# State space mixer in fp32: masks added in the exponent, the two directions' decays summed, states multiplied with C itself

## The chip, the cores and the metric

The kernel runs on 1 core of one Trainium2 chip. The metric is the device time of one execution in microseconds (us); "before" is the median of 3 runs. The engines are TensorE (PE; its weight loads are PEld), VectorE (DVE), ScalarE (ACT), GpSimd (POOL) and SyncE (SP, which issues most DMAs).

## The reference, cut to what matters

The model has two layers; the change lies in the second layer's mixer, a bidirectional state space mixer (Mamba-2 form) over 512 latent tokens that start from a state built by 256 context tokens. There are 8 groups of 4 heads; a head has 64 channels and a group one B and one C of 128 state rows per token. Per direction and chunk:

```python
acum = jnp.cumsum(dtc * a, axis=2)
seg = acum[:, :, :, None] - acum[:, :, None, :]
decay = jnp.exp(jnp.where(causal, seg, -jnp.inf))
cb = jnp.einsum('nblgk,nbsgk->nblsg', cc, bc)
y_diag = jnp.einsum('nblsgh,nbsghp->nblghp', cb[..., None] * decay * dtc[:, :, None], xc)
...
y = y_d + jnp.einsum('blgk,bghpk->blghp', c_i, hs) * jnp.exp(a_i)[..., None]
...
y = (yf + yb + dsk * xs).reshape(bsz, t, SSD_INNER) * jax.nn.silu(z.astype(F32))
yg = yg * lax.rsqrt(jnp.mean(yg * yg, axis=-1, keepdims=True) + RMS_EPS)
```

`yf` and `yb` are the two directions; the norm runs over the 256 channels of a group. An output projection, a residual and an expert layer with 16 experts follow.

## The kernel before, in words

One program in the Tile framework; the framework places each engine's instructions in an order of its own from the program's order and a simulated timeline, and each engine then works through its queue in that order. Tiles come from pools with a fixed number of buffers; an instruction or load that needs a buffer waits until its last reader is done. PSUM has 8 banks: tags "mm" (3), "tp" (2), "at" (2) and "o" (1).

The mixer (L1389 to L1655) works on chunks of 128 tokens: 4 latent chunks and 2 of context. **Setup** (L1414 to L1476): the step sizes dt of 64 head-directions, their cumulated decays `ac` (64 x 768), written to DRAM as `acd` (L1468); `ad` = ac - ln dt; both transposed to `acT` and `adT` (tokens on partitions); the chunk ends go to DRAM and come back broadcast as `eb` (L1469), whose exponential ScalarE takes (L1471).

**Per group** (loop at L1517): the input projection on TensorE for x, B, C and later z, each product in three passes of split fp32r (the weights are split by ScalarE and VectorE, L721 and L722); the 5-tap convolution, four taps of it on VectorE (L1492); transposes; `cb`, the product of B and C of a chunk, with each direction's triangle multiplied in by VectorE (L1563); `xw`, x times its weight, on GpSimd (L1572); the chunk states `st` in a chain of three steps over TensorE, GpSimd (L1585) and VectorE (L1589, L1597).

**Per block** m of two heads (128 channels; 2 blocks a group) and direction d, L1613 to L1642: `R` is a load of two heads' cumulated decays, broadcast to all partitions (L1621, issued by ScalarE's queue; 2 buffers). Eight VectorE instructions of 128x128 make the exponent `mt` = min(R, acT) - adT (L1627), ScalarE takes the exponential (L1629), VectorE multiplies with `cb` (L1630), and 8 matmuls with 64 columns of weights each add x·mt to `py`. ScalarE also takes exp(R) (L1631), GpSimd multiplies it with C (L1632), and 8 matmuls of the same shape add st·R to `py`. Every fp32 matmul shows as two records in the trace.

After both directions VectorE reads `py` (L1646), multiplies with the gate (L1648), and ScalarE squares (L1649). A group's norm (`norm_group`, L1499) runs in the middle of the next group's projection: 8 matmuls with a column of ones sum the squares, then a power on GpSimd, transposes, and the scaled y goes to DRAM `yd`, from which the output projection (`project`, L1673) reads it back. All of the helper `mm`'s matmuls have line L77.

## Time and profile before

| | us |
|---|---|
| median of 3 runs | 2380.43 |
| lowest and highest | 2377.44 and 2381.2 |
| profiled execution, its own time | 2382.69 |
| span of the profiled execution | 2381.0 |
| its mean granted TensorE clock | 0.979 of full speed |

The rows below come from the profiled execution, so a sum over them stands against its own time. Busy time says how long an engine worked in a stretch; the chain of waits says which work the end waited for; "idle before" beside a group of instructions says how long its engine stood still before them and which instruction ended that.

### The profile page before, as it was taken

The page shows a single profiled execution, that of the slowest core. Times are in us where ns is not written, and L with a number is a line of the kernel's source. Part 1 is how long each engine was busy: PE and PEld are TensorE (multiplying, and loading weights), DVE is VectorE, ACT ScalarE, POOL GpSimd, SP SyncE. Part 2 cuts the span into 40 slices and gives each one's busy share as a digit, 9 for nine tenths or more (in the row PEclk, how much of TensorE's full clock was granted, in tenths as well). Part 3 has the DMA queues.
Part 4 walks back from the last instruction along what each step waited for, and adds up shares of the span by engine and source line. Part 5 has one row for each costly group of instructions (what it writes and reads, how often), then busy time and mean ns, then how long its engine had stood idle before and what let it go on. Part 6 is the DMA issues. An engine that isn't in the chain of part 4 may idle for free. (4 is left out here: it accounts for less than half of the span.)

```text
span 2381.0 us, 37608 instructions
## 1 busy us (share of the span) xinstructions
PE 2228.0 (94%) x15522; PEld 1392.7 (58%) x15522; DVE 1273.3 (53%) x2231; ACT 847.0 (36%) x1408; POOL 513.9 (22%) x383
## 2 busy tenths in 40 slices
PE   7999999989999999999988999999989999988886
PEld 6888887877344444444476787777768633322222
DVE  5566476635243443343577888888885512222224
ACT  4446455522242343343463444434443211111111
POOL 1000044421121222221222434334442000000001
PEclk9999999999899999999998999999999899999999
DMA  8554311249999999999733232322256999999996
GB/s 270 162 163 150 103 37 55 71 137 338 352 368 366 370 379 387 368 383 356 271 101 108 91 124 92 94 84 89 89 178 243 358 366 418 419 419 418 419 418 264
DMA packets 253707, 587.94 MB, mean 247 GB/s; under 512 B 14240, under 2 KB 129056, under 8 KB 253536
## 3 DMA queue, kind: packets, MB, share of 16 engines
q1 hardware_dynamic: 240960, 548.44, 61.2%
q0 software_dynamic: 5280, 18.88, 3.1%
q10 hardware_dynamic: 7296, 18.22, 2.3%
q8 instruction: 122, 2.00, 0.3%
q14 instruction: 49, 0.40, 0.1%
HBM read 560.99 MB, written 24.51 MB: 246 GB/s over the span
## 5 line engine op out<-in xcount | busy, mean ns | idle before, releaser
L77 PE MATMUL mm<-w_moe,xs 128*32 128x512 f32 (+1 forms) x4080 | 596.3, 597 | 20.7 <-DMA w_moe<-in_w_dram 20.7
L77 PE MATMUL mm<-xh,w_s 128*128 128x512 f32 (+2 forms) x1824 | 479.1, 357 | 4.4 <-ACT z L1087 3.7
L77 PEld LDWEIGHTS mm<-w_moe,xs 128*32 128x32 f32 (+1 forms) x4080 | 171.1, 116 | 397.9 <-issue 336.4
L77 PEld LDWEIGHTS mm<-xh,w_s 128*128 128x128 f32 (+1 forms) x1824 | 307.3, 189 | 55.9 <-issue 8.2
L77 PE MATMUL mm<-xl,w_s 128*128 128x512 f32 (+1 forms) x912 | 296.4, 357 | 0.0
L77 PEld LDWEIGHTS mm<-xl,w_s 128*128 128x128 f32 x912 | 160.0, 189 | 24.7 <-issue 4.2
L77 PE MATMUL at<-w_s,hT_h 128*96 128x512 f32 x480 | 162.8, 405 | 1.6 <-POOL w_s L514 1.1
L514 DVE TENSOR_TENSOR w_s<-w_moe,w_s 128x1024 fp32r<-128x1024 f32 x90 | 126.9, 1432 | 62.9 <-ACT w_s L513 62.6
L1492 DVE SCALAR_TENSOR_TENSOR acc<-u,cwh,acc 128x770 f32<-128x770 f32 (+1 forms) x128 | 149.2, 1173 | 15.2 <-ACT acc L1489 13.9
L514 POOL TENSOR_TENSOR w_s<-w_moe,w_s 128x1024 fp32r<-128x1024 f32 x30 | 75.0, 2499 | 334.1 <-ACT w_s L513 257.7
L513 ACT CAST w_s<-w_moe 128x1024 fp32r<-128x1024 f32 x120 | 124.4, 1049 | 46.7 <-PE at L77 22.1
L1632 POOL TENSOR_TENSOR R<-R,cT 128x1024 f32<-128x1024 f32 x32 | 101.3, 3179 | 132.2 <-ACT R L1631 109.6
L77 PE MATMUL at<-w_moe,o 128*64 128x512 f32 x512 | 119.9, 599 | 8.9 <-DMA w_moe<-in_w_dram 7.3
L479 DVE TENSOR_TENSOR ha<-mm,ha 128x512 f32<-128x512 f32 x16 | 11.1, 691 | 217.6 <-PE mm L77 216.9
L77 PEld LDWEIGHTS at<-w_s,hT_h 128*96 128x96 f32 x480 | 75.1, 161 | 59.3 <-issue 22.6
L478 ACT ACTIVATE ha<-mm 128x512 f32<-128x512 f32 x16 | 9.6, 597 | 260.1 <-PE mm L77 260.1
L772 DVE TENSOR_TENSOR w_s<-w_raw,w_s 128x1024 fp32r<-128x1024 f32 x56 | 75.7, 1357 | 46.3 <-ACT w_s L771 46.1
L77 PE MATMUL at<-w_s,hT_l 128*96 128x512 f32 x240 | 94.2, 392 | 0.0
L1572 POOL TENSOR_TENSOR xw<-xk,weT 128x256 f32<-128x256 f32 x80 | 72.3, 935 | 98.5 <-ACT xk L1550 98.5
L647 DVE TENSOR_TENSOR ha<-mm,ha 128x512 f32<-128x512 f32 x16 | 11.1, 691 | 147.7 <-PE mm L77 147.7
L77 PE MATMUL mm<-w_s,xh 128*128 128x256 f32 x480 | 89.2, 290 | 0.2
L646 ACT ACTIVATE ha<-mm 128x512 f32<-128x512 f32 x16 | 9.6, 597 | 223.6 <-PE mm L77 223.6
(463 smaller groups left out, 3680.1 us busy)
## 6 DMA issues: line engine op xcount, KB each, us to landing
w_moe<-in_w_dram SPq DMA_DIRECT2D x380, 1024.0 KB
w_ada<-in_ada_w_dram SPq DMA_DIRECT2D x34, 1024.0 KB
w_raw<-in_ssd_w_in_dram SPq DMA_DIRECT2D x16, 1024.0 KB
R<-acd ACTq DMA_DIRECT2D x32, 512.0 KB
spare<-in_ada_w_dram SPq DMA_DIRECT2D x14, 1024.0 KB
w_raw<-in_ab_w_in_dram SPq DMA_DIRECT2D x12, 1024.0 KB
w_raw<-in_ssd_w_in_dram SPq DMA_DIRECT2D x16, 512.0 KB
w_raw<-in_ssd_w_out_dram SPq DMA_DIRECT2D x8, 1024.0 KB
```

The lines of the kernel that those rows point to most:

```text
L77: return T.matmul(o, l, r, start=start, stop=stop, skip_group_check=True, **k)
L478: S.activation(ha, B[0], AF.Silu)
L479: V.tensor_tensor(ha, B[1], ha, ALU.mult)
L513: S.copy(wh, w2[:, kk, :])
L514: (G if k % 4 == 3 else V).tensor_tensor(wl, w2[:, kk, :], wh.bitcast(F32), ALU.subtract)
L646: S.activation(ha, B[0], AF.Silu)
L647: V.tensor_tensor(ha, B[1], ha, ALU.mult)
L772: V.tensor_tensor(wl, r, wh.bitcast(F32), ALU.subtract)
L1492: V.scalar_tensor_tensor(acc[:, :n], u[:, i:i + n], cwh[:, i * 32 + cblk:i * 32 + cblk + 1], acc[:, :n], op0=ALU.mult, op1=ALU.add)
L1572: G.tensor_tensor(xw[:, i, d, :].rearrange("p (h c) -> p h c", h=4), xk[:, i, :].rearrange("p (h c) -> p h c", h=4), we[:, i, d, :].unsque ...
L1632: G.tensor_tensor(R, R, cT.rearrange("p (a b) -> p a b", a=4).unsqueeze(1).to_broadcast([128, 2, 4, 128]), ALU.mult)
```

## The change

The triangle is no longer multiplied into `cb` but added to the exponent: `tri` holds 0 and -1e30. VectorE adds it to a whole `R` tile of 128x1024 at once, and ScalarE takes eight exponentials of 128x128 with `adN` = ln dt - ac as the bias. The two directions' decays are summed by VectorE before one product with the unmasked `cb` (copied from PSUM by ScalarE) and one set of 8 matmuls. The states are multiplied with C itself (4 matmuls with 128 columns of weights per direction, into an "at" or a "tp" bank), and VectorE scales that product by `E` = exp(ac), which the setup computes once, stores as `ead`, and each block loads broadcast to 64 partitions per head. GpSimd sums the two directions' E, adds the sum to y between VectorE's two instructions, and sums the squares of a group's two blocks, so that 4 matmuls do in place of 8. `R` has 3 buffers and is also the place of `mt`; `E` has 3.

```diff
--- before.py
+++ after.py
@@ -1389,14 +1389,15 @@
         w_in = A["ssd_w_in"]
         yd = dram.tile([16, 128, LAT], F32, name="yd")
         acd = dram.tile([64, LAT], F32, name="acd")
+        ead = dram.tile([64, LAT], F32, name="ead")
         lad = dram.tile([64, 4], F32, name="lad")
         with ExitStack() as sx:
             sp = sx.enter_context(tc.tile_pool(name="ssc", bufs=1, side="right"))
             tri = [sp.tile([128, 128], F32, name=f"stri{d}") for d in range(2)]
             for d in range(2):
                 sgn = 1 - 2 * d
-                G.memset(tri[d], 1.0)
-                G.affine_select(out=tri[d], in_=tri[d], pattern=[[sgn, 128]], compare_op=ALU.is_ge, fill=0.0,
+                G.memset(tri[d], 0.0)
+                G.affine_select(out=tri[d], in_=tri[d], pattern=[[sgn, 128]], compare_op=ALU.is_ge, fill=-1e30,
                                 base=0, channel_multiplier=-sgn)
             ones = sp.tile([128, 1], F32, name="ones")
             G.memset(ones, 1.0)
@@ -1405,8 +1406,7 @@
             V.tensor_scalar(cwh, vec("cw"), 0.5, None, op0=ALU.mult)
             V.tensor_scalar(cbh, vec("cb"), 0.5, None, op0=ALU.mult)
 
-            acT = sp.tile([128, NTL, 64], F32, name="acT")
-            adT = sp.tile([128, NTL, 64], F32, name="adT")
+            adN = sp.tile([128, NTL, 64], F32, name="adN")
             weT = sp.tile([128, NT, 64], F32, name="weT")
             eb = sp.tile([128, 64, 4], F32, name="eb")
             sp = sx.enter_context(tc.tile_pool(name="ssd", bufs=1, side="right"))
@@ -1415,8 +1415,8 @@
                 w = load_split(w_in[:, 6144:6208], 64)
             pl, pc = gemm_fm(w, 0, m=64)
             dt = sp.tile([64, TOK], F32, tag="xw", name="dt")
-            e_ = sp.tile([64, TOK], F32, tag="mt", bufs=2, name="dte")
-            l_ = sp.tile([64, TOK], F32, tag="mt", bufs=2, name="dtl")
+            e_ = sp.tile([64, TOK], F32, tag="R", bufs=3, name="dte")
+            l_ = sp.tile([64, TOK], F32, tag="R", bufs=3, name="dtl")
             ac = sp.tile([64, TOK], F32, tag="st", name="ac")
             msk = sp.tile([64, TOK], F32, tag="zs", name="dmask")
             na_ = sp.tile([64, 1], F32, name="nega")
@@ -1448,7 +1448,7 @@
                     if d:
                         o, i = o[:, ::-1], i[:, ::-1]
                     V.tensor_tensor_scan(o, msk[q, t0:t1], i, 0.0, ALU.mult, ALU.add)
-            V.tensor_tensor(ad, ac[:, :LAT], ad, ALU.subtract)
+            V.tensor_tensor(ad, ad, ac[:, :LAT], ALU.subtract)
             lat_ = sp.tile([64, 4], F32, name="la")
 
             for d in range(2):
@@ -1466,10 +1466,12 @@
             S.activation(l_, l_, AF.Exp)
             V.tensor_tensor(l_, l_, dt, ALU.mult)
             S.dma_start(out=acd[:, :], in_=ac[:, :LAT])
+            S.activation(msk[:, :LAT], ac[:, :LAT], AF.Exp)
+            S.dma_start(out=ead[:, :], in_=msk[:, :LAT])
             S.dma_start(out=eb.rearrange("p a b -> p (a b)"),
                         in_=lad.rearrange("a b -> (a b)").partition_broadcast(128))
             S.activation(eb, eb, AF.Exp)
-            for t, o, n in ((ac, acT, NTL), (ad, adT, NTL), (l_, weT, NT)):
+            for t, o, n in ((ad, adN, NTL), (l_, weT, NT)):
                 q = tp_bank([128, 8, 64])
                 for i in range(n):
                     tr(q[:, i, :], t[:, i * 128:(i + 1) * 128])
@@ -1501,8 +1503,7 @@
                 spare_bank = at_bank if g < 7 else lambda shape: bank("o", 1, shape)
                 pm = spare_bank([128, 4])
                 for c in range(4):
-                    for m in range(2):
-                        mm(pm[:, c:c + 1], sqs[m][:, c * 128:(c + 1) * 128], ones, m == 0, m == 1)
+                    mm(pm[:, c:c + 1], sqs[0][:, c * 128:(c + 1) * 128], ones, True, True)
                 r = rsqrt(pm, 4, 1.0 / 256)
                 pr_ = spare_bank([128, 4, 128])
                 for c in range(4):
@@ -1557,11 +1558,8 @@
                 for c in range(4):
                     cs = slice(c * 128, (c + 1) * 128)
                     mm(p[:, c, :], bT[:, cs], cT[:, cs], True, True)
-                cb = []
-                for d in range(2):
-                    t = sp.tile([128, 4, 128], F32, name=f"cb{d}")
-                    V.tensor_tensor(t, p, tri[d].unsqueeze(1).to_broadcast([128, 4, 128]), ALU.mult)
-                    cb.append(t)
+                cb = sp.tile([128, 4, 128], F32, name="cb")
+                S.copy(cb, p)
 
                 xw = sp.tile([128, NT, 2, 256], F32, name="xw")
                 we = weT.rearrange("p t (d g h) -> p t d g h", d=2, g=8)[:, :, :, g, :]
@@ -1614,41 +1612,52 @@
                     py = bank("o", 1, [128, 4, 128])
                     clear(py)
                     hm = slice(m * 128, (m + 1) * 128)
+                    def heads(c, w, r, last):
+
+                        for hh in range(2):
+                            mm(py[hh * 64:(hh + 1) * 64, c, :], w[:, hm][:, hh * 64:(hh + 1) * 64], r[:, hh, c, :], False, last)
+                    Es = []
                     for d in range(2):
-
+                        h = d * 32 + g * 4 + m * 2
+                        E = sp.tile([128, 4, 128], F32, name="E", bufs=3)
+                        for hh in range(2):
+                            S.dma_start(out=E[hh * 64:(hh + 1) * 64].rearrange("p a b -> p (a b)"),
+                                        in_=ead[h + hh, :].partition_broadcast(64))
+                        q = at_bank([128, 4, 128]) if d == 0 else tp_bank([128, 4, 128])
+                        for n in range(4):
+                            c = n if d == 0 else 3 - n
+                            mm(q[:, c, :], st[:, n, d, hm], cT[:, c * 128:(c + 1) * 128], True, True)
+                        V.tensor_tensor(E, q, E, ALU.mult)
+                        Es.append(E)
+                    G.tensor_tensor(Es[0], Es[0], Es[1], ALU.add)
+                    mts = []
+                    for d in range(2):
                         col = d * 32 + g * 4 + m * 2
-                        R = sp.tile([128, 2, 4, 128], F32, name="R", bufs=2)
+                        R = sp.tile([128, 2, 4, 128], F32, name="R", bufs=3)
                         S.dma_start(out=R.rearrange("p h a b -> p (h a b)"),
                                     in_=acd[col:col + 2, :].rearrange("h t -> (h t)").partition_broadcast(128))
-                        mt = sp.tile([128, 2, 4, 128], F32, name="mt", bufs=2)
+                        mt = R
+                        V.tensor_tensor(mt, R, tri[d][:, None, None, :].to_broadcast([128, 2, 4, 128]), ALU.add)
+
                         for hh in range(2):
                             for c in range(4):
-                                h = col + hh
-                                V.tensor_scalar(mt[:, hh, c, :], R[:, hh, c, :], acT[:, c, h:h + 1], adT[:, c, h:h + 1],
-                                                op0=ALU.min, op1=ALU.subtract)
-                        S.activation(mt, mt, AF.Exp)
-                        V.tensor_tensor(mt, mt, cb[d].unsqueeze(1).to_broadcast([128, 2, 4, 128]), ALU.mult)
-                        S.activation(R, R, AF.Exp)
-                        G.tensor_tensor(R, R, cT.rearrange("p (a b) -> p a b", a=4).unsqueeze(1).to_broadcast([128, 2, 4, 128]),
-                                        ALU.mult)
-
-                        def heads(c, w, r, last):
-                            for hh in range(2):
-                                mm(py[hh * 64:(hh + 1) * 64, c, :], w[:, hm][:, hh * 64:(hh + 1) * 64], r[:, hh, c, :], False, last)
-
-                        for c in range(4):
-                            heads(c, xk[:, c], mt, False)
-                        for n in range(4):
-                            heads(n if d == 0 else 3 - n, st[:, n, d], R, True)
+                                S.activation(mt[:, hh, c, :], mt[:, hh, c, :], AF.Exp, bias=adN[:, c, col + hh:col + hh + 1])
+                        mts.append(mt)
+                    V.tensor_tensor(mts[0], mts[0], mts[1], ALU.add)
+                    V.tensor_tensor(mts[0], mts[0], cb.unsqueeze(1).to_broadcast([128, 2, 4, 128]), ALU.mult)
+                    for c in range(4):
+                        heads(c, xk[:, c], mts[0], True)
                     y = sp.tile([128, LAT], F32, name="y", bufs=2)
                     sq = sp.tile([128, LAT], F32, name="ysq", bufs=2)
                     blk = g * 2 + m
                     V.scalar_tensor_tensor(y, xg[:, m, :LAT], vec("dsk", blk, 1), py.rearrange("p a b -> p (a b)"),
                                            op0=ALU.mult, op1=ALU.add)
+                    G.tensor_tensor(y, y, Es[0].rearrange("p a b -> p (a b)"), ALU.add)
                     V.scalar_tensor_tensor(y, y, 0.5, zs[:, m, :], op0=ALU.mult, op1=ALU.mult)
                     S.activation(sq, y, AF.Square)
                     sqs.append(sq)
                     ys.append(y)
+                G.tensor_tensor(sqs[0], sqs[0], sqs[1], ALU.add)
 
                 tail = lambda g=g, ys=ys, sqs=sqs: norm_group(g, ys, sqs)
                 more_ada(min(2, len(ada_left) - NL))
```

## Rows read from the trace of the kernel before

**Rows 1.** The page's part 1: busy us, share of the span, instructions, whole span.

```profile
PE 2228.0 (94%) x15522; PEld 1392.7 (58%) x15522; DVE 1273.3 (53%) x2231; ACT 847.0 (36%) x1408; POOL 513.9 (22%) x383
```

**Rows 2.** Busy by stretch: window, length; PE, PEld, DVE, ACT, POOL; granted clock, DMA share, GB/s.

```profile
1260.00:1300.00 40.00, 31.41 (x193) 22.39 (x192) 28.88 (x46) 14.84 (x25) 15.94 (x17) 0.83 0.33 94
...
1300.00:1768.00 468.00, 441.81 (x2927) 353.68 (x2928) 398.94 (x602) 203.60 (x302) 196.93 (x146) 0.99 0.32 102
...
1800.00:1920.00 120.00, 115.84 (x734) 84.53 (x734) 57.66 (x158) 34.60 (x68) 12.99 (x14) 0.94 0.81 304
...
1920.00:2300.00 380.00, 346.66 (x1510) 112.75 (x1508) 89.85 (x148) 44.52 (x84) 5.86 (x5) 1.00 1.02 418
```

**Rows 3.** The chain of waits, by line, 1300 to 1768 us (the view cuts it there).

```profile
by line: DVE acc L1492 18.2%; PE mm L77 13.2%; DVE mt L1627 12.3%; PE at L77 8.6%; DVE w_s L722 5.4%; DMA R<-acd 4.8%; POOL xw L1572 4.3%; DVE mt L1630 4.0%; PE o L77 3.8%; issue 3.6%; DMA w_raw<-in_ssd_w_in_dram 2.4%; DVE xg L1497 1.8%; AC
```

**Rows 4.** Timeline of one group, VectorE, then GpSimd: start, us, instruction.

```profile
1587.39 4.24 DVE L1627 TENSOR_SCALAR mt<-R,acT,adT 128x128 f32<-128x128 f32 x8
...
1603.43 2.14 DVE L1627 TENSOR_SCALAR mt<-R,acT,adT 128x128 f32<-128x128 f32 x8
...
1588.12 2.40 POOL L1632 TENSOR_TENSOR R<-R,cT 128x1024 f32<-128x1024 f32 x1 [13.06 <-ACT R L1631]
```

**Rows 5.** Groups by line and form, VectorE, 1260 to 1800: busy, mean ns, idle before.

```profile
L1492 DVE SCALAR_TENSOR_TENSOR acc<-u,cwh,acc 128x770 f32<-128x770 f32 x88 | 108.0, 1228 | 13.6 <-ACT acc L1489 12.5
...
L1627 DVE TENSOR_SCALAR mt<-R,acT,adT 128x128 f32<-128x128 f32 x256 | 83.4, 397 | 5.0 <-DMA R<-acd 4.8
...
L1630 DVE TENSOR_TENSOR mt<-mt,cb 128x1024 f32<-128x1024 f32 x32 | 49.2, 1554 | 0.4 <-ACT mt L1629 0.4
...
L1563 DVE TENSOR_TENSOR cb<-at,stri 128x512 f32<-128x512 f32 x16 | 10.2, 680 | 3.5 <-PE at L77 3.5
```

**Rows 6.** One line's instructions (L1492 from 1240 to 1800): min/median/max ns.

```profile
L1492 DVE SCALAR_TENSOR_TENSOR acc<-u,cwh,acc x127: 740/1022/3155, 1240.0 to 1750.5; 128x770 f32<-128x770 f32 x95, 128x512 f32<-128x512 f32 x32
...
L1630 DVE TENSOR_TENSOR mt<-mt,cb x32: 1207/1216/3372, 1289.5 to 1787.0; 128x1024 f32<-128x1024 f32 x32
```

**Rows 7.** Groups by form, GpSimd: L1632, and L1338 of the first layer.

```profile
L1632 POOL TENSOR_TENSOR R<-R,cT 128x1024 f32<-128x1024 f32 x32 | 101.3, 3179 | 132.2 <-ACT R L1631 109.6 <-DVE cT L1497 12.7 <-PE at L1509 4.3
...
L1338 POOL TENSOR_TENSOR x_res<-x_res,ytmp 128x512 f32<-128x512 f32 x6 | 7.5, 1282 | 6.8 <-DVE ytmp L1337 6.8
```

**Rows 8.** Groups by form, TensorE's matmuls in PSUM, 1260 to 1800 us.

```profile
L77 PE MATMUL o<-R,st 128*64 128x128 f32 x512 | 39.5, 279 | 2.5 <-POOL R L1632 2.4
...
L77 PE MATMUL o<-mt,xk 128*64 128x128 f32 x512 | 35.5, 277 | 7.1 <-DVE mt L1630 7.1
...
L77 PE MATMUL at<-ones,ysq 128*128 128x1 f32 x112 | 13.3, 239 | 0.0
...
L77 PE MATMUL at<-cT,bT 128*128 128x128 f32 x64 | 10.9, 323 | 3.5 <-DVE cT L1497 3.5
```

**Rows 9.** Groups by form, ScalarE, whole span.

```profile
L1629 ACT ACTIVATE mt<-mt 128x1024 f32<-128x1024 f32 x32 | 33.9, 1060 | 26.9 <-DVE mt L1627 26.7
...
L1631 ACT ACTIVATE R<-R 128x1024 f32<-128x1024 f32 x32 | 33.4, 1045 | 0.0
...
L1579 ACT COPY st<-at 128x512 f32<-128x512 f32 x8 | 4.7, 585 | 29.8 <-PE at L77 29.8
...
L1233 ACT ACTIVATE mix<-tp,vecT 128x128 fp32r<-128x128 f32 x12 | 3.4, 371 | 8.9 <-DVE ostg L1231 8.9
```

**Rows 10.** R's load: its issues (min/median/max ns), then one on the chain.

```profile
L1621 ACTq DMA_DIRECT2D R<-acd x32: 321/326/446, 1256.0 to 1774.2; - x32
...
1579.79 3.43 DMA R<-acd
```

**Rows 11.** Timeline of the setup's end, ScalarE: start, us, idle before.

```profile
1268.67 0.42 ACT L1471 ACTIVATE eb<-eb 128x256 f32<-128x256 f32 x1 [8.11 <-DMA eb<-lad]
```

**Rows 12.** Timeline of one group, VectorE: its two instructions on y.

```profile
1581.49 0.75 DVE L1646 SCALAR_TENSOR_TENSOR y<-xg,vecT,o 128x512 f32<-128x512 f32 x1 [0.54 <-PE o L77]
...
1584.03 0.68 DVE L1648 SCALAR_TENSOR_TENSOR y<-y,zs 128x512 f32<-128x512 f32 x1
```

## The prediction, made before the change was run

> **What bounds the kernel now.** I read the page's shares first: TensorE is busy 94% of the whole span, VectorE 53% [rows 1]; that average hides stages with different limits. The busy time by stretch [rows 2] separates them. In the main part of the state space mixer (1300 to 1768 us, about seven of its eight groups) TensorE is busy 441.8 of 468 us and VectorE 398.9 (85%); ScalarE (203.6) and GpSimd (196.9) are under half, DMA at 0.32. From 1920 us on it is another kernel: DMA share 1.02 at 418 GB/s, the stream of the experts' weights, after 304 GB/s from 1800 on. That stream begins as the mixer gives its buffers back, so I let an earlier end of the mixer shift it one to one.
>
> Next the chain of waits within the main part [rows 3]. Two engines share it: VectorE (convolution taps 18.2%, the mask's exponents L1627 12.3%, the product with C·B L1630 4.0%, weight split 5.4%) and TensorE (13.2% + 8.6% + 3.8%). So the stage is a near tie: TensorE is idle for only 26 us, and what it waits for is mostly VectorE. A cut has to hit both. VectorE's time is partly not its own: eight exponent instructions took 4.24 us while GpSimd's R·C ran for 2.40 us beside them, and 2.14 us at a time without it [rows 4]. GpSimd's product took 2.1 us out of VectorE.
>
> The units below: 8 groups, 16 blocks (group, m), 32 block-directions.
>
> **VectorE, removed:** L1627 83.4, L1630 49.2, two masked copies of C·B (L1563) 10.2: 142.8 us [rows 5]. **Added:** 32 products E = q·E, 128x512 with one input from PSUM, the shape and operands of L1563: 32 x 10.2/16 = 20.4 us. 32 mask additions, 16 sums of decays, 16 products with C·B: 64 instructions of 128x1024 from SBUF, L1630's shape: 64 x 1.21 (its least duration [rows 6]) = 77 to 64 x 1.54 (busy time over count) = 99 us. The spread is the stall beside GpSimd; half of GpSimd's mixer product work goes, so I take the middle, 1.38: 88 us. Net 142.8 - 20.4 - 88 = 34 us (24 to 45). The 770-wide taps, of which 88 averaged 1.228 us against a median of 1.022 [rows 5, 6], carry 18 us of stall; I give back a third, 6 us. VectorE: **-40 us** (-24 to -54).
>
> **GpSimd, removed:** 32 R·C, 101.3 us [rows 7]. Added: per block the sum of the two Es and y + E, per group the sum of squares: 40 additions of 128x512. The same shape takes 1.28 us at L1338; half of the mean R·C, 3.18, is 1.59. That makes 51 to 64 us, and I take 51. GpSimd is under half busy: price 0 by itself, and less time in VectorE's way. The Trainium skill, SBUF — State Buffer, Who interferes with whom, says that a GpSimd instruction reading SBUF and a VectorE instruction with two SBUF inputs exclude each other for a whole instruction; the pair in [rows 4] agrees (2.1 us lost beside 2.40). By that rule the E products are exempt, and the 40 additions could still hold VectorE for 51 us, against 77 for 32 x 2.40 before, a relief of at most 26 us.
>
> **TensorE.** The products with the states do not shrink by being fewer: R·st took 39.5 us for 512 records, 0.077 each, because each has only 64 columns of weights and two run abreast [rows 8]. st·C has 256 records with full width; priced from C·B (10.9/64 = 0.170, the same shape, waits included) they take 44 us, from the squares' column sums (13.3/112 = 0.119) 30 us. I take 37. Summing both decays before the product with x halves the o<-mt group: -17.8. One pass over squares in place of two: -6.7. Net 37 - 39.5 - 17.8 - 6.7 = **-27 us** (-20 to -34).
>
> **ScalarE.** Gone: two 128x1024 exponentials per block-direction, 67.3 us. Added: 256 exponentials of 128x128 with a bias from SBUF. No such row; nearest by shape is L1233, 128x128 with a pointer operand, 0.371 us: 95 us. The lower end is one 1024-wide pass, 33.9 us. A copy of C·B per group, 8 x 0.585 = 4.7 us [rows 9]. Its queue also issues 64 more DMAs (E in two halves) at 0.326 us: 21 us [rows 10]. Balance -8 to +53, near the upper end. Even +53 leaves ScalarE near 250 of 468 us, so I price it at 0; if the cover went, the exponentials of a block would add 16 x 0.371 - 2 x 1.06 = 3.8 us per block, 61 us. The E loads (64 x 128 KB, 8.4 MB) meet a DMA share of 0.32: 0, unless late (below).
>
> **Buffers and setup.** R and mt become one pool of three, of which one comes free after the sum of decays; that should loosen the waits for R's DMA (4.8% of the chain), which I don't count. The psum bank of y is held for 8 products and not 32. The new wait is the E product's for E's load: it holds an at and a tp bank, which the states' sums, the norm and the next group's transposes want too, and on VectorE the mask additions stand behind it (rival 2). In the setup one exponential and one more store stand before the eb load on ScalarE's queue, whose consumer already waited 8.1 us [rows 11]: between 0 and about 1 us each way (two transposes' worth of work goes); I take +1. Conditions on the last group: its norm gets two GpSimd hops, some 3 us, under 100 us of output projection.
>
> **The sum.** Two ways. If TensorE keeps its 26 us of idle time, the stage loses TensorE's 27 us. By the chain: L1627 and L1630 have 16.3% of 468 = 76 us on it, 57% of their 133 us; 57% of VectorE's 40 is 23. TensorE's o products have 3.8% = 18 us on it, a quarter of 75; a quarter of 27 is 7. Together 30. I take 28, less 1 for the setup: **27 us**. The profiled execution took 2382.69 us (span 2381.0), 2.3 above the median of 2380.43; by its own time 2355.7, against the median **2353 us**.
>
> **Rivals.**
> 1. *Larger gain.* VectorE is the real limit and TensorE's idle time shrinks too. For it: 54 us is VectorE's upper bound and [rows 3] gives it most of the chain. Against: TensorE after the cut still needs some 418 of 468 us. With all but a few of the 26 us of idle gone, -45: 2335 us. [...]
> 2. *Hidden or eaten by transfers.* Each E tile needs its own two loads, issued in order on ScalarE's queue and waiting for a buffer that the previous y + E frees. R's load is 3.43 us on the chain when it is there, 22 us in all [rows 3, 10]. If E's loads get a like share, +22: 2376 us, no change or a small gain.
> 3. *Slower: y goes through GpSimd.* VectorE's queue is in order; between its two instructions on y now stands a GpSimd addition. Before, they were 2.54 us apart start to start with other work between [rows 12]. If VectorE stands still for the addition and for one GpSimd instruction ahead of it (1.28 + 1.28 = 2.6 us, 16 times) it loses 41 us, and with it what its queue holds behind: the next taps and mask additions, for which TensorE waits. 2353 + 41 = 2394 us. It decides from 1.7 us per block (27/16). Against: the order has other VectorE work to place there.
> 4. *It doesn't do what it says:* the E product is no cheaper for TensorE (priced so already); were VectorE's 64 instructions all stalled as L1630 was and no tap relieved, VectorE's net is 24, its part of the chain 14 in place of 23, and the time about 2361.
>
> **Chances.** Forecast with rival 4 (gains of 15 to 40 us, 2340 to 2365) 0.52; larger gain 0.14; transfers 0.16, of which 0.07 still a gain over 0.2%; slower 0.18. A measurement of this kernel can tell about 0.2% (4.8 us) from no change. Faster 0.52 + 0.14 + 0.07 = 0.73; same 0.09; slower 0.18. The range leaves out a tenth at each end: 2333 to 2390, from just past rival 1 to most of rival 3.
>
> **What would show it.** Right: per-stage busy time of VectorE down by 35 to 50 us and of TensorE by 20 to 34, the 1300 to 1768 work some 25 us shorter, the start of the 418 GB/s stretch earlier by as much, GpSimd some 50 us less. Wrong: VectorE idle before the y·z product with GpSimd as releaser (rival 3); VectorE or TensorE waiting for E's DMA, or ScalarE's queue standing at E's issues (rival 2); exponentials on the chain; TensorE's granted clock, 0.99 now, falling because it idles more, as between 1260 and 1300 us, where it was 0.83 with TensorE busy 31.4 of 40 us.

## The result and the profile after

The changed kernel took **2350.41 us** (median of 4 runs, 2342.2 to 2354.0) against 2380.0 for the kernel before: ratio **0.9869, 95% interval 0.9848 to 0.9891**, 30 us less. Its profiled execution took 2348.53 us, with a span of 2346.8 us.

Part 1 of the page after, in the columns of [rows 1]:

```profile
PE 2195.4 (94%) x14942; PEld 1377.4 (59%) x14942; DVE 1222.5 (52%) x2022; ACT 866.9 (37%) x1609; POOL 483.8 (21%) x391
```

Over the whole span VectorE has 51 us less, TensorE 33, GpSimd 30, and ScalarE 20 more. To see where the time went, a stretch with fixed ends is needed: from the first to the last y·z product (L1648 before, L1656 after), sixteen in each kernel. Busy time by stretch, columns as in [rows 2]; first the kernel before:

```profile
1310.80:1796.40 485.60, 457.55 (x3040) 365.36 (x3039) 416.97 (x629) 214.14 (x315) 205.39 (x149) 0.99 0.33 106
```

and after, the same stretch and then the experts' stream of [rows 2]:

```profile
1310.80:1762.10 451.30, 432.54 (x2538) 355.87 (x2539) 360.29 (x430) 222.27 (x464) 173.32 (x156) 0.97 0.40 129
...
1885.00:2265.00 380.00, 346.99 (x1510) 112.78 (x1506) 89.83 (x148) 44.77 (x84) 5.86 (x5) 1.00 1.02 418
```

The stretch begins at the same microsecond, 1310.80, and is 34.3 us shorter; the span is 34.2 us shorter. So all of the gain lies here, and what follows only moves to an earlier start, with the DMA share (1.02) and 418 GB/s it had. TensorE gave up 25 us of work and 9 of its 28 idle us (485.60 - 457.55 = 28.1; now 18.8). VectorE gave up 57 and is now busy 80% of the stretch, after 86%.

The groups by line and form, 1230 to 1780 us: count, then busy, mean ns, idle before. They answer to [rows 5], [rows 7] to [rows 9]:

```profile
L1494 DVE SCALAR_TENSOR_TENSOR acc<-u,cwh,acc 128x770 f32<-128x770 f32 x96 | 108.6, 1134 | 9.9 <-ACT acc L1491 8.8
...
L1644 ACT ACTIVATE R<-R,adN 128x128 f32<-128x128 f32 x256 | 78.9, 389 | 71.2 <-DVE R L1640 71.0
...
L1640 DVE TENSOR_TENSOR R<-R,stri 128x1024 f32<-128x1024 f32 x32 | 41.6, 1299 | 26.4 <-DMA R<-acd 26.2
...
L1655 POOL TENSOR_TENSOR y<-y,E 128x512 f32<-128x512 f32 x16 | 29.1, 1819 | 1.3
...
L1632 POOL TENSOR_TENSOR E<-E 128x512 f32<-128x512 f32 x16 | 28.0, 1752 | 84.5 <-DVE E L1630 84.5
...
L77 PE MATMUL tp<-cT,st 128*128 128x128 f32 x128 | 22.9, 283 | 2.1 <-DVE st L1595 2.1
...
L1646 DVE TENSOR_TENSOR R<-R 128x1024 f32<-128x1024 f32 x16 | 22.7, 1421 | 2.7 <-ACT R L1644 2.7
...
L1647 DVE TENSOR_TENSOR R<-R,cb 128x1024 f32<-128x1024 f32 x16 | 19.7, 1271 | 4.7 <-ACT cb L1562 4.7
...
L77 PE MATMUL o<-R,xk 128*64 128x128 f32 x256 | 19.3, 282 | 0.0
...
L77 PE MATMUL at<-cT,st 128*128 128x128 f32 x128 | 16.9, 275 | 0.0
...
L1660 POOL TENSOR_TENSOR ysq<-ysq 128x512 f32<-128x512 f32 x8 | 13.5, 1682 | 23.6 <-ACT ysq L1657 23.6
...
L1630 DVE TENSOR_TENSOR E<-at,E 128x512 f32<-128x512 f32 x16 | 11.0, 685 | 4.5 <-PE at L77 4.4
...
L1630 DVE TENSOR_TENSOR E<-tp,E 128x512 f32<-128x512 f32 x16 | 10.9, 684 | 10.9 <-DMA E<-ead 10.9
...
L77 PE MATMUL at<-ones,ysq 128*128 128x1 f32 x56 | 6.6, 239 | 0.0
```

The products with the states (tp and at <- cT,st) take 22.9 + 16.9 = 39.8 us where R·st took 39.5 [rows 8]: half as many instructions for the same time. The sum of decays halves the product with x (o<-R,xk, 19.3 us, after 35.5 [rows 8]).

The chain of waits, 1300 to 1733 us, as in [rows 3]:

```profile
by line: PE mm L77 37.9%; DVE acc L1494 12.3%; PE at L77 8.1%; DMA R<-acd 6.1%; DVE w_s L722 4.3%; DMA E<-ead 4.0%; issue 3.8%; PE o L77 2.3%; DVE R L1640 2.2%; DVE R L1646 1.6%; ACT R L1644 1.5%; PE tp L88 1.4%; PE tp L77 1.3%; DVE bT L149
```

The mask's two VectorE lines had 16.3% in [rows 3]; of the three that took their place the view shows two, 3.8% together (L1640, L1646); TensorE's projections (mm) went from 13.2% to 37.9%, and E's load is new with 4.0%. The table of waits after (waiter, releaser: us in total, times, longest) shows what VectorE now waits for, 1310.8 to 1762.1 us:

```profile
DVE R L1640 <- DMA R<-acd: 20.9, 16, 3.6
...
DVE E L1630 <- DMA E<-ead: 10.9, 3, 5.4
...
DVE y L1656 <- POOL y L1655: 2.4, 2, 1.2
```

In the kernel before, the same table has for R's load:

```profile
DVE mt L1627 <- DMA R<-acd: 3.1, 6, 0.9
```

So VectorE now waits 31.8 us for loads, where it waited 3.1; all of its idle time in the stretch went from 68.6 us to 91.0. The wait for GpSimd ahead of y·z, the slower rival's place, is 2.4 us.

### The profile page after: what moved, and what is told of

Same layout as the page of the kernel before. It is cut to its first block, busy times and chain, and to the rows that moved or that the text cites. A ratio compares the mean times of both kernels' runs of the same rounds, so it can differ in the third digit from the quotient of the medians.

```text
span 2346.8 us, 36580 instructions
## 1 busy us (share of the span) xinstructions
PE 2195.4 (94%) x14942; PEld 1377.4 (59%) x14942; DVE 1222.5 (52%) x2022; ACT 866.9 (37%) x1609; POOL 483.8 (21%) x391
## 5 line engine op out<-in xcount | busy, mean ns | idle before, releaser
L77 PE MATMUL mm<-w_moe,xs 128*32 128x512 f32 (+1 forms) x4080 | 596.6, 597 | 20.4 <-DMA w_moe<-in_w_dram 20.4
L1494 DVE SCALAR_TENSOR_TENSOR acc<-u,cwh,acc 128x770 f32<-128x770 f32 (+1 forms) x128 | 139.0, 1094 | 10.4 <-ACT acc L1491 9.3
L77 PEld LDWEIGHTS at<-w_s,hT_h 128*96 128x96 f32 x480 | 75.1, 161 | 59.3 <-issue 22.6
L1644 ACT ACTIVATE R<-R,adN 128x128 f32<-128x128 f32 x256 | 78.9, 389 | 71.2 <-DVE R L1640 71.0
L772 DVE TENSOR_TENSOR w_s<-w_raw,w_s 128x1024 fp32r<-128x1024 f32 x56 | 73.1, 1309 | 42.4 <-ACT w_s L771 42.3
```

The costliest lines, as they stand in the source:

```text
L77: return T.matmul(o, l, r, start=start, stop=stop, skip_group_check=True, **k)
L772: V.tensor_tensor(wl, r, wh.bitcast(F32), ALU.subtract)
L1494: V.scalar_tensor_tensor(acc[:, :n], u[:, i:i + n], cwh[:, i * 32 + cblk:i * 32 + cblk + 1], acc[:, :n], op0=ALU.mult, op1=ALU.add)
L1644: S.activation(mt[:, hh, c, :], mt[:, hh, c, :], AF.Exp, bias=adN[:, c, col + hh:col + hh + 1])
```

## The experiments

The ratio is always to the kernel before, run beside it on the same chip. In this section "gain" and "loss" are differences of medians.

**p1_squares**: the kernel before with only the squares' part of the change.

```diff
-                    for m in range(2):
-                        mm(pm[:, c:c + 1], sqs[m][:, c * 128:(c + 1) * 128], ones, m == 0, m == 1)
+                    mm(pm[:, c:c + 1], sqs[0][:, c * 128:(c + 1) * 128], ones, True, True)
...
+                G.tensor_tensor(sqs[0], sqs[0], sqs[1], ALU.add)
```

> The kernel before with one part alone: the two blocks' squares summed on GpSimd, one pass of column sums instead of two. Theory T (a part's gain is what it takes off TensorE's busy time): the at<-ones group falls from 13.6 to about 6.7 us, the time by 5 to 8 us, about 2373. Theory V (a part's gain is what it takes off VectorE's own instructions): VectorE gains nothing and meets 8 more GpSimd additions, no change, 2378 to 2384. Theory L (a part's gain is GpSimd's time that VectorE no longer stands beside): GpSimd gets 13 us more, 2380 to 2390.

Measured 2383.68 us, ratio 1.0008 (0.9997 to 1.0019): no change. The group by form, 1230 to 1830 us, has the halved work, 7.0 us where it was 13.3 [rows 8]:

```profile
L77 PE MATMUL at<-ones,ysq 128*128 128x1 f32 x56 | 7.0, 245 | 2.8 <-POOL ysq L1652 2.8
```

Counting the 6.3 us that TensorE is spared fails here. That they are worth nothing by themselves is not shown: the eight additions that take their place lie on GpSimd, and VectorE, whose instructions are the same, was busy for 5.7 us more between the first and the last y·z (416.97 before):

```profile
1314.10:1800.60 486.50, 456.80 (x2977) 364.72 (x2976) 422.66 (x630) 213.59 (x315) 218.16 (x156) 0.97 0.33 107
```

The two may cancel; the saving without the additions was not run.

**u1_no_squares**: the changed kernel with the squares as before.

```diff
-                    mm(pm[:, c:c + 1], sqs[0][:, c * 128:(c + 1) * 128], ones, True, True)
+                    for m in range(2):
+                        mm(pm[:, c:c + 1], sqs[m][:, c * 128:(c + 1) * 128], ones, m == 0, m == 1)
...
-                G.tensor_tensor(sqs[0], sqs[0], sqs[1], ALU.add)
```

> The changed kernel without the sum of squares on GpSimd (two passes of column sums again). T: TensorE +7 us, 2354 to 2360 against 2350. V: no change from 2350. L: GpSimd 13 us less, 2343 to 2350.

Measured 2350.74 us, 0.9882 (0.9866 to 0.9898), as the whole change. Adding the squares' part to the one kernel or taking it out of the other changes nothing that can be seen; both times TensorE's work and GpSimd's change together.

**p2_states**: the kernel before with only the states' part: C times the states, E from memory, no exp(R), no R·C. The masks and exponents stay as they were; R and the exponent share three buffers, as in the changed kernel.

```diff
+                        E = sp.tile([128, 4, 128], F32, name="E", bufs=3)
...
+                            mm(q[:, c, :], st[:, n, d, hm], cT[:, c * 128:(c + 1) * 128], True, True)
+                        V.tensor_tensor(E, q, E, ALU.mult)
...
-                        S.activation(R, R, AF.Exp)
-                        G.tensor_tensor(R, R, cT.rearrange("p (a b) -> p a b", a=4).unsqueeze(1).to_broadcast([128, 2, 4, 128]),
-                                        ALU.mult)
...
+                    G.tensor_tensor(y, y, Es[0].rearrange("p a b -> p (a b)"), ALU.add)
```

> The kernel before with one part alone: states multiply C itself, the product scaled by E, no exp(R) and no R.C on GpSimd (R and the exponent share three buffers, as in the changed kernel). T: TensorE's 39.5 us for R.st become about 39.8, so no change, 2374 to 2384. V: VectorE gets 32 more products, 22 us, of which about half show: 2385 to 2400. L: GpSimd's mixer products go from 101 us to about 57, VectorE stands less, 2355 to 2370.

Measured 2370.26 us, 0.9958 (0.9943 to 0.9972): a gain of 11 us, at the low end of what theory L expected.

**p3_masks**: the kernel before with only the masks' part: mask added ahead of the exponential, decays summed, one product with C·B. exp(R) and R·C stay.

```diff
-                                V.tensor_scalar(mt[:, hh, c, :], R[:, hh, c, :], acT[:, c, h:h + 1], adT[:, c, h:h + 1],
-                                                op0=ALU.min, op1=ALU.subtract)
-                        S.activation(mt, mt, AF.Exp)
-                        V.tensor_tensor(mt, mt, cb[d].unsqueeze(1).to_broadcast([128, 2, 4, 128]), ALU.mult)
+                        V.tensor_tensor(mt, R, tri[d][:, None, None, :].to_broadcast([128, 2, 4, 128]), ALU.add)
...
+                                S.activation(mt[:, hh, c, :], mt[:, hh, c, :], AF.Exp, bias=adN[:, c, col + hh:col + hh + 1])
...
+                    V.tensor_tensor(mts[0], mts[0], mts[1], ALU.add)
+                    V.tensor_tensor(mts[0], mts[0], cb.unsqueeze(1).to_broadcast([128, 2, 4, 128]), ALU.mult)
```

> The kernel before with one part alone: triangle added to the exponent, eight exponentials with bias on ScalarE, the two decays summed, one product with C.B and one set of eight matmuls; exp(R) and R.C on GpSimd stay. T: the o<-mt matmuls halve, 35.5 to about 19 us, 2360 to 2368. V: VectorE loses 143 us and gets 84, net -59, of which 57% on the chain: 2340 to 2352. L: GpSimd unchanged, and 64 two-input instructions in place of 32 beside it: no change, 2374 to 2384.

Measured 2386.68 us, 1.003 (1.0017 to 1.0043): a **loss** of 6 us, which lies in no theory's range. Three groups by form of this kernel, 1230 to 1830 us:

```profile
L1627 POOL TENSOR_TENSOR R<-R,cT 128x1024 f32<-128x1024 f32 x32 | 82.2, 2576 | 117.4 <-ACT R L1626 86.6 <-PE mm L77 13.6 <-DVE rs_t L138 10.3
...
L1637 DVE TENSOR_TENSOR mt<-mt,cb 128x1024 f32<-128x1024 f32 x16 | 34.5, 2157 | 4.0 <-ACT cb L1560 3.7
L1636 DVE TENSOR_TENSOR mt<-mt 128x1024 f32<-128x1024 f32 x16 | 24.3, 1522 | 14.3 <-ACT mt L1624 14.3
```

The product with C·B takes 2.157 us at a mean, where the same product takes 1.271 (L1647) in the changed kernel, which has no R·C. VectorE's busy time as a whole fell even so, and the time rose. By stretch, first to last y·z product, and the chain of waits in it:

```profile
1308.50:1800.80 492.30, 460.41 (x2843) 368.74 (x2842) 377.86 (x410) 260.38 (x535) 195.89 (x149) 0.96 0.32 106
```

```profile
by line: PE mm L77 26.9%; DVE acc L1491 9.7%; PE at L77 9.5%; ACT mt L1624 8.1%; issue 5.7%; DMA R<-acd 4.7%; DVE w_s L722 4.1%; DVE mt L1621 3.7%; POOL xw L1568 3.3%; PE o L77 2.8%; DVE mt L1636 2.6%; ACT R L1626 2.5%; DVE mt L1637 1.8%; A
```

VectorE is busy for 39 us less than in the kernel before (416.97), yet the stretch is 6.7 us longer, with TensorE idle for 31.9 us and the eight exponentials (L1624) on the chain for 8.1%. So VectorE's busy us are not time by themselves: it also matters what they stand ahead of.

Squares 0, states -11 and masks +6 don't add up to -30: the parts depend on each other. The next two runs ask whether R·C is the link.

**n1_before_no_rc**: the kernel before, less its GpSimd product R·C, so that C is left out of the result.

```diff
-                        G.tensor_tensor(R, R, cT.rearrange("p (a b) -> p a b", a=4).unsqueeze(1).to_broadcast([128, 2, 4, 128]),
-                                        ALU.mult)
```

> The kernel before without the product R.C on GpSimd (the matmuls with the states take exp(R) itself, so C is left out of the result). It takes 101 us off GpSimd and nothing off TensorE, ScalarE or VectorE's own instructions. B: VectorE stands less, TensorE becomes the bound, the gain of the states part: 2355 to 2370. Rival S (what GpSimd holds does not matter; the states part gains by other means, such as a shorter chain into the bank of y): 2376 to 2384.

Measured **2349.75 us**, 0.9873 (0.9839 to 0.9908). That is below the range expected. One line of GpSimd's, 32 instructions that have no piece on the chain of the kernel before between 1310.8 and 1796.4 us, was worth 31 us, as much as the whole change. This kernel's groups on VectorE, 1230 to 1830 us:

```profile
L1492 DVE SCALAR_TENSOR_TENSOR acc<-u,cwh,acc 128x770 f32<-128x770 f32 x96 | 101.0, 1053 | 13.9 <-ACT acc L1489 12.7
L1627 DVE TENSOR_SCALAR mt<-R,acT,adT 128x128 f32<-128x128 f32 x256 | 70.9, 350 | 7.9 <-DMA R<-acd 7.9
L722 DVE TENSOR_TENSOR w_s<-w_raw,w_s 128x1024 fp32r<-128x1024 f32 x46 | 57.3, 1249 | 7.5 <-ACT w_s L721 7.4
L1630 DVE TENSOR_TENSOR mt<-mt,cb 128x1024 f32<-128x1024 f32 x32 | 39.2, 1246 | 0.5 <-ACT mt L1629 0.5
...
L1563 DVE TENSOR_TENSOR cb<-at,stri 128x512 f32<-128x512 f32 x16 | 10.3, 684 | 4.3 <-PE at L77 4.3
```

and two of the kernel before, same view and stretch (that of L1492 in [rows 5] has 88 of the 96):

```profile
L1492 DVE SCALAR_TENSOR_TENSOR acc<-u,cwh,acc 128x770 f32<-128x770 f32 x96 | 116.1, 1210 | 15.1 <-ACT acc L1489 13.9
...
L722 DVE TENSOR_TENSOR w_s<-w_raw,w_s 128x1024 fp32r<-128x1024 f32 x46 | 65.4, 1423 | 10.5 <-ACT w_s L721 10.5
```

Not one VectorE instruction differs between the two kernels, yet the four groups take 15.1 + 12.5 + 8.1 + 10.0 = 45.7 us less. The product with an operand in PSUM (L1563) keeps its time, 0.684 us against 0.680 [rows 5]. The Trainium skill, SBUF — State Buffer, Who interferes with whom, says that only VectorE instructions with two SBUF inputs, or in a two-port mode that the single-input form (as L1627) can enter, contend with GpSimd's reads: these groups agree; that L1627 ran in such a mode no run shows. One pair in the kernel before, GpSimd's product and a tap with two SBUF inputs (median 1.022 [rows 6]):

```profile
1593.75 2.38 POOL L1632 TENSOR_TENSOR R<-R,cT 128x1024 f32<-128x1024 f32 x1 [3.23 <-ACT R L1631]
...
1593.83 3.12 DVE L1492 SCALAR_TENSOR_TENSOR acc<-u,cwh,acc 128x770 f32<-128x770 f32 x1
```

L1563 is a control: in the trace of the kernel before, ten of its sixteen ran beside an R·C and took 0.683 us at a mean, the other six 0.676. By stretch, first to last y·z product:

```profile
1311.00:1764.00 453.00, 448.89 (x3037) 363.27 (x3036) 370.17 (x629) 215.31 (x315) 106.20 (x119) 1.00 0.35 113
```

TensorE is now idle for 4.1 us, where it was 28.1: what is left of its work fills the stretch. VectorE is busy for 46.8 us less (370.17 after 416.97), and the stretch is 32.6 us shorter. The run takes away more than GpSimd's hold on VectorE, though: the matmuls with the states no longer wait for a step between ScalarE's exponential and them, and R's buffer comes free earlier. How much of the 31 us is VectorE's time it doesn't separate.

**n2_masks_no_rc**: p3_masks, less the same product, C again left out of the result.

```diff
-                        G.tensor_tensor(R, R, cT.rearrange("p (a b) -> p a b", a=4).unsqueeze(1).to_broadcast([128, 2, 4, 128]),
-                                        ALU.mult)
```

> The masks part alone, again without the product R.C on GpSimd (C left out of the result in the same way). B: GpSimd's product is what hid the gain of the masks part, so with it gone both gains show, 2338 to 2356. Rival S (the masks part alone is slow by its longer way through ScalarE, eight exponentials and then exp(R) per block-direction, which this kernel keeps): 2372 to 2390.

Measured 2337.99 us, 0.9826 (0.9792 to 0.9859): 49 us under p3_masks and 12 under n1_before_no_rc. By stretch:

```profile
1304.20:1751.10 446.90, 442.21 (x2816) 353.76 (x2815) 333.82 (x408) 259.73 (x534) 116.33 (x119) 0.99 0.35 116
```

VectorE's busy time is 44 us under that of p3_masks, and TensorE's idle time falls from 31.9 us to 4.7. The masks' part is thus no loss in itself, only beside R·C. Whether it is R·C's hold on VectorE's two-input instructions there, or that R·C gives R back later, these runs don't separate.

**i1_pe_twice**: the changed kernel, the products of states made twice (TensorE +27.9 us: 67.7 in place of 39.8, by the two groups below).

```diff
-                            mm(q[:, c, :], st[:, n, d, hm], cT[:, c * 128:(c + 1) * 128], True, True)
+                            for _ in range(2):
+                                mm(q[:, c, :], st[:, n, d, hm], cT[:, c * 128:(c + 1) * 128], True, True)
```

> The changed kernel with every product of states and C made twice into the same bank: TensorE gets the group's 40 us once more, nothing else is added. Theory B (the changed stage is bound by TensorE, after the states part took GpSimd's product out of VectorE's way): 30 to 42 us longer than 2350, so 2380 to 2392. Theory V (bound by VectorE): 0 to 12 us longer, 2350 to 2362. Both near bound: 15 to 30 us longer.

Measured 2373.58 us, 0.9969 (0.9951 to 0.9986): 23 us over the changed kernel, 0.83 of what was put in. The two groups, 1230 to 1830 us:

```profile
L77 PE MATMUL tp<-cT,st 128*128 128x128 f32 x256 | 36.5, 278 | 0.0
L77 PE MATMUL at<-cT,st 128*128 128x128 f32 x256 | 31.2, 275 | 0.0
```

**i2_vector_more**: the changed kernel, with 64 spare VectorE products of 128x512 from PSUM (43.8 us).

```diff
+                        Ej = sp.tile([128, 4, 128], F32, name="Ej")
+                        for _ in range(2):
+                            V.tensor_tensor(Ej, q, E, ALU.mult)
```

> The changed kernel with two more VectorE products q.E into a spare tile before each real one: 64 instructions of 0.64 us, 41 us more on VectorE, one input from PSUM so that GpSimd does not stand beside them. B: 0 to 15 us longer, 2350 to 2365. V: 25 to 41 us longer, 2375 to 2391.

Measured 2394.67 us, 1.0066 (1.0043 to 1.0088): 44 us more, all of what was put in and above the range expected. By stretch:

```profile
1314.60:1809.10 494.50, 452.09 (x2586) 368.63 (x2587) 395.82 (x491) 225.31 (x462) 166.67 (x156) 0.95 0.38 123
```

TensorE's idle time goes from 18.8 to 42.4 us (494.50 - 452.09), and its granted clock from 0.97 to 0.95. VectorE, busy 80%, sets the time in full where this work stands, and TensorE nearly so (i1_pe_twice). The spare products also hold the PSUM tile that TensorE wants and the E tile that the next load wants; spare work at another place on VectorE was not run. That TensorE alone bounds the changed kernel is excluded.

**x1_no_e_loads**: the changed kernel without E's loads, scaled by a tile of ones: the decay is left out of the result.

```diff
-                            S.dma_start(out=E[hh * 64:(hh + 1) * 64].rearrange("p a b -> p (a b)"),
-                                        in_=ead[h + hh, :].partition_broadcast(64))
-                        V.tensor_tensor(E, q, E, ALU.mult)
+                        V.tensor_tensor(E, q, Ec, ALU.mult)
```

> The changed kernel without the 64 loads of E: the products of states and C are scaled by one tile of ones that stays (the decay is left out of the result). Every other instruction stays. Theory D (the changed kernel gives part of its gain back to loads on ScalarE's queue: VectorE stands 21 to 26 us before the mask additions until R has landed, because E's issues, 0.55 us each, and waits for E's buffers stand ahead of R's): 10 to 25 us shorter, 2325 to 2340. Rival H (the loads are hidden, VectorE's busy time is what counts): no change, 2344 to 2356.

Measured 2341.28 us, 0.9835 (0.981 to 0.986): 9 us less than the changed kernel, just under the 10 to 25 expected if the loads cost time. The two intervals overlap by a little (that of the changed kernel begins at 0.9848), so the size is not firm. This takes the issues along with the loads, 64 at a median 0.547 us on ScalarE's queue, by the changed kernel's one line (least/median/most ns):

```profile
L1624 ACTq DMA_DIRECT2D E<-ead x64: 452/547/1676, 1256.6 to 1752.0; - x64
```

**r1_masks_first**: the changed kernel with R's loads, masks and exponentials ahead of E in each block.

```diff
+                    mts = []
+                    for d in range(2):
+                        col = d * 32 + g * 4 + m * 2
+                        R = sp.tile([128, 2, 4, 128], F32, name="R", bufs=3)
...
                     Es = []
...
-                    mts = []
-                    for d in range(2):
-                        col = d * 32 + g * 4 + m * 2
-                        R = sp.tile([128, 2, 4, 128], F32, name="R", bufs=3)
...
```

The loop that these lines begin is moved whole, unchanged.

> The changed kernel with the two directions' R loads, mask additions and exponentials placed ahead of E's loads and products in each block; the same instructions in another order. D: R no longer queues behind E, 4 to 15 us shorter, 2335 to 2346. H: no change, 2344 to 2356.

Measured 2349.99 us, 0.9865 (0.9835 to 0.9894): no change. But the framework, which orders each engine's queue itself, kept the old order: in the trace every engine runs the changed kernel's instructions in the changed kernel's order, but for two neighbours on ScalarE's queue, and the 32 issues for R and the 64 for E alternate as they did. VectorE's waits for loads, 1313.8 to 1763.1 us, are the changed kernel's too (20.9 and 10.9):

```profile
DVE R L1626 <- DMA R<-acd: 20.5, 14, 4.4
...
DVE E L1643 <- DMA E<-ead: 9.6, 3, 4.9
```

So this run is the changed kernel once more. Whether the waits would go with R's loads issued first stays open.

**v1_adds_on_vector**: the changed kernel with the block's two GpSimd additions on VectorE.

```diff
-                    G.tensor_tensor(Es[0], Es[0], Es[1], ALU.add)
+                    V.tensor_tensor(Es[0], Es[0], Es[1], ALU.add)
...
-                    G.tensor_tensor(y, y, Es[0].rearrange("p a b -> p (a b)"), ALU.add)
+                    V.tensor_tensor(y, y, Es[0].rearrange("p a b -> p (a b)"), ALU.add)
```

> The changed kernel with the sum of the two E products and y + E on VectorE, 32 additions of 128x512 from SBUF, about 0.69 us each, 22 us; GpSimd loses 57 us and y no longer passes through it. If VectorE's own time counts as the doubled product suggested (44 us for 41): plus 22, less what GpSimd's 57 us took out of VectorE (at the 31 us per 101 of the kernel before: 18), so 2350 to 2358. If instead the pass of y through GpSimd is what holds the block (the prediction's rival 3): 2325 to 2342.

Measured 2345.48 us, 0.9854 (0.983 to 0.9878): between the two ranges expected, and not told apart from the changed kernel. Its groups on VectorE, 1230 to 1830 us, show where the additions' time went:

```profile
L1494 DVE SCALAR_TENSOR_TENSOR acc<-u,cwh,acc 128x770 f32<-128x770 f32 x96 | 101.5, 1065 | 15.8 <-ACT acc L1491 15.5
L722 DVE TENSOR_TENSOR w_s<-w_raw,w_s 128x1024 fp32r<-128x1024 f32 x46 | 58.9, 1283 | 6.1 <-ACT w_s L721 6.1
L1640 DVE TENSOR_TENSOR R<-R,stri 128x1024 f32<-128x1024 f32 x32 | 39.7, 1241 | 15.7 <-DMA R<-acd 15.7
...
L1646 DVE TENSOR_TENSOR R<-R 128x1024 f32<-128x1024 f32 x16 | 19.5, 1218 | 1.9 <-ACT R L1644 1.9
L1647 DVE TENSOR_TENSOR R<-R,cb 128x1024 f32<-128x1024 f32 x16 | 18.9, 1218 | 7.2 <-ACT cb L1562 7.2
```

and the one of the changed kernel that is not shown above, same view and stretch:

```profile
L722 DVE TENSOR_TENSOR w_s<-w_raw,w_s 128x1024 fp32r<-128x1024 f32 x46 | 64.4, 1406 | 6.1 <-ACT w_s L721 5.7 <-PE at L77 0.2
```

The five groups take 7.1 + 5.5 + 1.9 + 3.2 + 0.8 = 18.5 us less than in the changed kernel. The 32 additions take 21.9 us on VectorE (0.68 each). They nearly pay for themselves by what they no longer take from VectorE on GpSimd.

**w1_e_from_r**: what these runs suggest. R already holds the sums whose exponentials are E, so ScalarE makes E from R before the mask goes in, and E's store and 64 loads go; the two additions are on VectorE. The result is the same.

```diff
-                            S.dma_start(out=E[hh * 64:(hh + 1) * 64].rearrange("p a b -> p (a b)"),
-                                        in_=ead[h + hh, :].partition_broadcast(64))
+                        E = sp.tile([128, 4, 128], F32, name="E", bufs=4)
+                        for hh in range(2):
+                            S.activation(E[hh * 64:(hh + 1) * 64], R[hh * 64:(hh + 1) * 64, hh], AF.Exp)
...
-                    G.tensor_tensor(Es[0], Es[0], Es[1], ALU.add)
+                    V.tensor_tensor(Es[0], Es[0], Es[1], ALU.add)
...
-                    G.tensor_tensor(y, y, Es[0].rearrange("p a b -> p (a b)"), ALU.add)
+                    V.tensor_tensor(y, y, Es[0].rearrange("p a b -> p (a b)"), ALU.add)
```

> The changed kernel without E's loads and without the ead store, with the same result: ScalarE makes E from R before the mask is added (two exponentials of 64x512 per block-direction, some 0.55 us each, 35 us more of ScalarE), R first in each block, and the two additions of E and y on VectorE. If the loads cost what their removal showed (9 us) and the additions on VectorE keep their 5 us: 2333 to 2342. If ScalarE's 35 us stand in the way of the mask's exponentials: 2345 to 2360.

Measured **2341.22 us** (2337.17 to 2342.65), 0.9833 (0.981 to 0.9856): 41 us less than the kernel before, and by the medians 9 less than the changed one, with intervals that overlap by a little. It reaches x1_no_e_loads, which left the decay out. From v1_adds_on_vector, which has the additions on VectorE alone, it can't be told apart, so what E made from R is worth by itself is not shown. The table of waits has no load in VectorE's longest places any more, 1307.7 to 1749.5 us:

```profile
DVE w_s L722 <- ACT w_s L721: 18.2, 12, 3.6
...
DVE R L1627 <- ACT E L1624: 10.1, 2, 5.1
```

The first is the weight split behind ScalarE, the second the mask behind the new exponentials. The chain of waits in this stretch, though, is nearly all TensorE's:

```profile
by line: PE mm L77 65.2%; PE at L77 12.7%; PE o L77 4.3%; PE tp L77 3.6%; PE tp L88 2.7%; DMA w_raw<-in_ssd_w_in_dram 1.2%; ACT E L1624 1.2%; POOL xw L1567 1.1%; ACT R L1631 0.9%; DVE acc L1491 0.7%; issue 0.7%; ACT w_s L721 0.7%; PE at L15
```

So by the chain TensorE's own work, 88% of it, is what comes next, and ScalarE's three lines have under 3%.

## Why the prediction was right

2353 us was forecast and 2350.41 measured: 30 us gained where 27 were expected. The likeliest case is the one that came; the sum was good, the reasons beneath it only in part. That the terms below missed in opposite directions and met so near is partly luck.

**VectorE, -40 predicted.** The masks' additions, decay sums and products took 41.6 + 22.7 + 19.7 = 84.0 us (88 said), E's products 21.9 (20.4 said). The taps of 770 fell from 116.1 to 108.6, 7.5 us (6 said). That makes 142.8 - 84.0 - 21.9 + 7.5 = 44 us. The step holds. The stretch gave 57; part of that is its edges, since 6 of the 32 mask additions now run ahead of it, where 2 of the 32 old masks did. The taps' stall was read from a median of 1.022 us that mixes both widths [rows 6]; the 18 us by it are 15.1 by n1_before_no_rc. And the pair of [rows 4] is not of the two-input form that the sentence beside it is about: L1627 has one tile as input. A tap beside R·C, 3.12 us against 1.022, is such a pair.

**TensorE, -27 predicted.** st·C took 39.8 us (37 said), o<-mt went from 35.5 to 19.3, the ones from 13.3 to 6.6. That is -22.6 by these groups; the stretch gave 25. That fewer instructions are not less time here was right.

**ScalarE.** The exponentials were busy 78.9 us (95 said), 0.308 each: they follow closely enough for their mean durations, 0.389, to overlap. E's issues took 35 us at the median of 0.547, where 0.326 each, 21 in all, was said from R's loads [rows 10]. The two errors cancel: 78.9 - 67.3 + 4.7 + 35 = +51, by the upper end said.

**GpSimd, 51 to 64 predicted, mis-sized.** The 40 additions took 29.1 + 28.0 + 13.5 = 70.6 us, 1.77 each. The low end came from L1338, 1.28 [rows 7]. There VectorE was busy for 4.6 of 7.5 us (533.8 to 541.3), but with products that read one operand from PSUM (`ytmp`, L1337). The range's upper end, half of R·C, was nearer.

**Setup, +1 predicted.** The first dt is 2 us earlier after the change (1229.9 against 1231.9) and the first y·z at the same microsecond, so setup with the first block took 2 us longer.

**The sum: where the steps failed.** Two ways were given, and both came to about the right figure.
- "If TensorE keeps its 26 us of idle time, the stage loses TensorE's 27 us" failed: the idle time shrank by 9 us, and the stretch lost 34. In the changed kernel 28 us more on TensorE cost 23 (i1_pe_twice); the 6 to 7 us of the squares brought nothing, but there GpSimd's work changed with them (p1_squares, u1_no_squares).
- The chain's way, where 57% of VectorE's 40 us counted, gave 30. No share of busy time holds: 44 us put on VectorE in the changed kernel cost 44 (i2_vector_more), and 39 us less in p3_masks gained nothing. The change also got 28.7 us of waits for loads, for which the forecast had 0; taking E's loads away returned about 9 us.
- "GpSimd ... price 0 by itself, and less time in VectorE's way" has the direction right, but sizes neither side. n1_before_no_rc shows 45.7 us of VectorE's time beside R·C, nearly half of the 101.3 us that R·C was busy [rows 7], and 31 us of the kernel's. The block's two additions that came in its place took 18.5 us back (v1_adds_on_vector). What was left in the change was near what was said: 7.5 us at the taps, 1.0 at the weight split (65.4 to 64.4).

So the change is better told as: leaving out R·C brings 31 us; what takes its place (E's products 22 us on VectorE, 57 us of additions on GpSimd, loads and issues) costs 20 of them, since the states' part alone gains 11; and the masks' part, a loss of 6 beside R·C, brings 20 once R·C is gone (p2_states 2370.26 against u1_no_squares 2350.74), or 12 without E's part (n1_before_no_rc against n2_masks_no_rc). That R·C is what ties the parts together these runs show; that it does so by VectorE's time alone is argued.

**The signs named.** TensorE's fall of 25 us in the stretch lies within the 20 to 34 named; VectorE's 57 is above the 35 to 50, GpSimd's 32 (205.39 - 173.32) well under the 50. Two of the signs of being wrong came as well: VectorE waits for E's DMA (10.9 us), and the granted clock fell from 0.99 to 0.97, though TensorE idles less and not more.

**The rivals.** A larger gain (2335) didn't come, since 18.8 us of TensorE's idle time stayed. Transfers (+22) were right in kind: E's loads and their issues cost about 9 us, not 22. Slower through GpSimd (+41) was not borne out: VectorE waited 2.4 us for y + E, and v1_adds_on_vector, without that hop, can't be told apart. That the change doesn't do what it says (2361) didn't come either.

## What to carry to other kernels

A GpSimd instruction with two SBUF inputs beside a loaded VectorE is priced by leaving it out once: here GpSimd's share of busy time said 0, and the run said 31 us. What is put in its place is priced the same way. Run the parts of a change one by one and also without the suspected link, since parts that share an engine don't add up (0, -11 and +6 made -30). Where a small tile is loaded by broadcast and its content can be made from one that is there already, making it is worth a run; here it came to some 9 us, barely clear of noise. Where a framework orders the queues itself, compare the order in the trace before reading "no change" from a reordered program.

## What was not expected of the hardware

- A load broadcast to 64 partitions held ScalarE's queue longer to issue (median 0.547 us) than one to 128 partitions with twice the rows (0.326 [rows 10], and the same in the changed kernel).
- GpSimd's hold on VectorE goes both ways: its 128x512 addition took 1.77 us at a mean in this stage and 1.28 in the first layer [rows 7], beside VectorE products with an operand in PSUM; R·C took 3.18 [rows 7] beside the old masks and 2.58 beside the new.
- TensorE's granted clock, a mean over time at its two levels (1.2 and 2.4 GHz), did not follow the idle time of the stretch alone: 1.00 with 4.1 us idle (n1_before_no_rc) and 0.95 with 42.4 (i2_vector_more), but 0.97 with 18.8 (after) against 0.99 with 28.1 (before). How the idle time is spread was not varied.
